# Two modulation blocks move from the out projection into the FFN up projection, with a new order of the first weight sums and activation sums

## The chip, the cores and the metric

The kernel runs on one core of one Trainium2 chip. The metric is the time on the device of one execution, in microseconds, as the median of several runs. The core has five engines with an instruction stream each: TensorE (PE, matrix products), VectorE (DVE), ScalarE (ACT), GpSimd (POOL) and SyncE (SP, which here only issues transfers). They wait for one another through semaphores. An engine takes its own stream in order, so whatever stands behind a waiting instruction waits as well.

## The reference

One decoder layer on a sequence of 1024 tokens of width 1024, in float32. A conditioning vector `c` gives six vectors of 1024 numbers each, by one product with `w_mod`:

```python
c_act = jax.nn.silu(c)
mod = c_act @ w_mod[l] + b_mod[l]
sh1, sc1, gt1, sh2, sc2, gt2 = [m[:, None, :] for m in jnp.split(mod, N_MOD, axis=-1)]
h = rms_norm(x, norm_mix[l]) * (1.0 + sc1) + sh1
p = h @ w_in[l]                      # split to three head groups: gMLP, RG-LRU, RWKV-7
y = jnp.concatenate([y_a, y_b, y_c], axis=-1) @ w_out[l]
x = x + gt1 * y
h = rms_norm(x, norm_ffn[l]) * (1.0 + sc2) + sh2
x = x + gt2 * conv_glu_ffn(h, ffn_w_up[l], ffn_conv_w[l], ffn_conv_b[l], ffn_w_down[l])
return rms_norm(x, norm_final)
```

`conv_glu_ffn` is `gate, val = split(h @ w_up)`, a causal convolution of three taps over time on `gate`, then `(silu(gate) * val) @ w_down`, with an inner width of 2816. The last modulation vector `gt2` is first read after the down projection's first product.

## The kernel before

**Precision.** Every float32 operand of a large product is split in two parts, a rounded one (`...h`, an ACT cast, L231) and the rest (`...l`, a DVE or POOL subtraction, L232). A product is three matmuls: high by high, high by low, low by high (L249 to L251, and L1124 to L1126 in the up projection). A matmul covers 128 x 128 weights and 512 tokens; the sequence is two halves f = 0 and 1 of 512 tokens (H).

**Modulation.** The product with `w_mod` is done in 12 blocks of 4 columns of `modc` each (`mod_block`, L279). A block has four loads of 512 KB (`wm`, L284). For each of the two halves of a load, DVE multiplies by a number of silu(c) and adds to `macc` (L292 for the first, L294 for the other seven); PE then sums over the partitions with four matmuls of one column (`pm`, L299), and DVE adds the bias (L300, `modc`). Blocks 4 to 9 are done inside the mixer. Blocks 10 and 11 give `gt2`, and wait in a list `modq`, four entries a block; `mod_rest(n)` takes the next n entries. A load takes one of three slots of the pool `wraw`, which the weights of the out projection, the up projection and `y` use as well. Slots are handed on in program order.

**Out projection.** For f = 0 and then 1, for 8 tiles k of the output (`out_tile`, L1027): x is loaded (L1029), the weights are loaded and split (`wr_wo`, `wh_wo`, `wl_wo`), 24 matmuls give `po`, DVE updates x (L1034), SP stores it (L1035), and ACT squares it for the next norm. `y_in` (L1018) loads what the mixer has stored (`yd`) and splits it. The table `MSTEP` says how many modulation entries run behind each of the 16 tiles: 4 for block 10 and 4 for block 11.

**FFN input.** `h2_in` (L1051) normalises x. The up projection multiplies 2 x 2 blocks (two halves of the tokens, two halves of the inner dimension) with seven products in place of eight, for tiles 1 to 21; tile 0 is done plainly. For that, sums of activation blocks T1 to T4 are formed on DVE for four chunks q (L1065 to L1068: T1, T3, T2, T4), and each is split in its parts: T2, T1 and T4 in the same loop, T3 in a loop behind it. T1 needs no T4; T2 is built on T1; T4 on T2.

**FFN up projection.** Each of 21 tiles has two raw weight blocks, `wr_ug` (gate) and `wr_uv` (value). `Up.first` (L1153) does the product `pA` with the block "11", and `gate` the product with "21", the convolution for f = 0 (`g`, L1141 to L1150). `Up.rest` (L1188) forms the weight sums in place, S3, S1, S2, S4 (L1201 to L1204, DVE or POOL by a table), splits them, and does the products `pB` (T2 by S2), `pD` (T3 by S3), `pC` (T1 by S1), `pD` again (T4 by v1) and `pC` again ("22" by S4): 84 matmuls a tile with `first` and `gate`. DVE reads the sums off PSUM: `p1` (L1211), `u` (L1214, L1218), `c` (L1221, L1222), `p1` again (L1225); the convolution for f = 1 follows, and two stores to `gd`. From tile 1 to 3, `first` has run before (NAHEAD = 3); tiles 4 to 20 ("late") have the gate's product between `pD` and `pC`.

**Order.** The code names the engine of each operation; a scheduler fixes each engine's order from the order of the code and its own estimates when the kernel is built. So a small edit moves instructions on every engine.

Of the kernel before, what the change touches and what calls it, by code (L numbers as in the profile page):

```python
# [14 lines left out]
ALU = mybir.AluOpType  # L15
# [6 lines left out]
H = 512  # L22
# [27 lines left out]

NAHEAD = 3
MAP = False
MSTEP = (0, 0, 0, 0, 0, 0, 1, 0, 1, 0, 0, 2, 1, 2, 0, 1)
FBLK = [(0, 4), (4, 10), (10, 16), (16, 18), (18, 22)]
NF2 = 3
NT2, NTB, _ = 7, 9, 5
# [96 lines left out]
def trunk(ctx: ExitStack, tc: tile.TileContext, xT, wmod, w_in, w_out, w_up, w_down,  # L153
          par, const, sgu_ln, sgu_wT, sgu_b, lora, g2w, lruw, outT):
    nc = tc.nc
    V, A, G, T = (Ordered(tc, e) for e in (nc.vector, nc.scalar, nc.gpsimd, nc.tensor))
    SY = nc.sync
# [69 lines left out]
    def eng(key, d):  # L227
        return {"V": V, "G": G, "A": A}[ENG.get(key, d)]
# [79 lines left out]
    yd = drp.tile([KT, P, S], F32, name="yd")  # L308
# [213 lines left out]
    def tb(nm):  # L522
        return r2.tile([P, H], F32, tag="tb", name=nm, bufs=NTB)

    def yout(kt, f, src):
        SY.dma_start(yd[kt, :, f * H:f * H + H], src)


    def c_tile(f, wi, idx, o, nm):
# [20 lines left out]
    def rwkv(j, f, stages):  # L550
# [13 lines left out]
        k = c_tile(f, 2 + 3 * j, 3 + j, t2(f"k{n}"), f"k{j}")  # L564
# [205 lines left out]
        def finish():  # L770

            mv = r1.tile([P, 3, 8], F32, tag="mv", name=f"mv{n}")
            sq = r2.tile([P, 8, 64], F32, tag="o", name=f"osq{n}", bufs=1)
            m_, s_, rs = mv[:, 0, :], mv[:, 1, :], mv[:, 2, :]
            V.reduce_sum(m_.unsqueeze(2), O, mybir.AxisListType.X)
            V.tensor_scalar(m_, m_, 1.0 / 64, None, ALU.mult)
            V.tensor_tensor(O, O, m_.unsqueeze(2).broadcast_to([P, 8, 64]), ALU.subtract)
            A.activation(sq, O, AF.Square)
            V.reduce_sum(s_.unsqueeze(2), sq, mybir.AxisListType.X)
            V.tensor_scalar(rs, s_, 1.0 / 64, GN_EPS, ALU.mult, ALU.add)  # L780
            rs = rsqrt(rs, 8, f"o{n}")
            yield
            eng("on", "V").tensor_tensor(O, O, rs.unsqueeze(2).broadcast_to([P, 8, 64]), ALU.mult)
            ps = mp.tile([P, 4, 2, 64], F32, tag="m", name=f"po{n}")
            for i in range(4):
                T.transpose(ps[:, i, :, :].rearrange("p a b -> p (a b)"),
                            O[:, 2 * i:2 * i + 2, :].rearrange("p a b -> p (a b)"), ident)
            o = r2.tile([P, H], F32, tag="o", name=f"o{n}", bufs=1)
            for hh in range(2):
                r_ = slice(64 * hh, 64 * hh + 64)  # L790
                for par_ in range(2):
                    A.activation(ch(o)[r_, par_:8:2, :], ps[64 * par_:64 * par_ + 64, :, hh, :], AF.Identity,
                                 scale=col("rwkv_ln_w", j)[r_], bias=col("rwkv_ln_b", j)[r_])
            eng("obv", "V").tensor_tensor(o, o, bv, ALU.add)
            ps = mp.tile([P, H], F32, tag="m", name=f"pgt{n}")
            T.matmul(ps, g2s[:, jc], sgg, start=True, stop=True)
            V.tensor_tensor(o, o, ps, ALU.mult)
            yout(5 + j, f, o)
            yield

        stages.update({f"L{j}{f}": lanes(), f"M{j}{f}": chain(), f"E{j}{f}": finish()})
# [208 lines left out]
    x1 = [[None] * KT, [None] * KT]  # L1010
# [31 lines left out]
    def parts(key, q, src, new, sh=None):  # L1042

        hi, lo = B[key, q] = tuple(new(f"{key}_{q}{p}") for p in "hl")
        if sh is None:
            split(src, hi, lo, eng("l" + key, "V"))
        else:
            A.activation(hi, src, AF.Identity, bias=sh)
            V.scalar_tensor_tensor(lo, src, sh, hi.bitcast(F32), ALU.add, ALU.subtract)

    def h2_in(f, acc):  # L1051

        rb = sumsq_bcast(acc, mp, f1, "rb", f"n2{f}", 1)
        yield
        hn = x1[f]
        sh = [modc[:, 24 + k:25 + k] for k in range(KT)]
        for q in range(4):
            for i, new in enumerate((hnew, hnew) if f == 0 else (anew, gnew)):
                k = q + 4 * i
                V.scalar_tensor_tensor(hn[k], hn[k], sg2[:, k:k + 1], rb, ALU.mult, ALU.mult)  # L1060
                parts(f"{i + 1}{f + 1}", q, hn[k], new, sh[k])
                yield
        for q in range(4 * f):
            b11, b21, b12, b22 = x1[0][q], x1[0][q + 4], hn[q], hn[q + 4]
            eng("T1", "V").tensor_tensor(b11, b12, b11, ALU.subtract)  # L1065
            eng("T3", "G").tensor_tensor(b12, b22, b12, ALU.subtract)
            eng("T2", "V").tensor_tensor(b22, b22, b11, ALU.subtract)
            eng("T4", "G").tensor_tensor(b21, b21, b22, ALU.subtract)  # L1068
            parts("T2", q, b22, anew, sh[q + 4])
            parts("T1", q, b11, anew)  # L1070
            parts("T4", q, b21, gnew)
            yield
        for q in range(4 * f):
            parts("T3", q, hn[q], anew, dsh[:, q:q + 1])
            yield
# [17 lines left out]
    for k in range(KT):  # L1093
        sq0 = out_tile(0, k, acc2[0])
        if k == 5:
            y_in(1)
        mod_rest(MSTEP[k])
    for k in range(KT):
        sq1 = out_tile(1, k, acc2[1])
        if k == 1:  # L1100
            h2 = h2_in(0, sq0)
            next(h2)
        mod_rest(MSTEP[8 + k])
        for _ in range((0, 1, 1, 2, 2, 2, 0, 0)[k]):
            next(h2)
    rp.close()
# [8 lines left out]
    def accp(nm):  # L1115
        return next(turn).tile([P, H], F32, tag="acc", name=nm)
# [15 lines left out]

    class Up:
        def __init__(self, ft):
            self.ft, self.raw = ft, None

        def conv(self, f, src):
            ft = self.ft
# [46 lines left out]
            V.tensor_tensor(g, g, ps[1], ALU.mult)  # L1185
            SY.dma_start(gd[ft, :, f * H:f * H + H], g)

        def rest(self, late):  # L1188
            ft = self.ft
            g = self.raw or raw_in(ft, f"ub{ft}")  # L1190
            v = raw_in(FT + ft, f"uv{ft}")
# [14 lines left out]
            wparts("S3", g0)  # L1206
            wparts("S1", v0)
            wparts("S4", g1)
            psB, psD, psC = accp(f"pB{ft}"), accp(f"pD{ft}"), accp(f"pC{ft}")
            prod(psB, w["S2"], "T2", True)  # L1210
            V.tensor_tensor(self.p1, self.p1, psB, ALU.add)  # L1211
            prod(psD, w["S3"], "T3", True)
            u3 = f2(f"u3{ft}")
            V.tensor_tensor(u3, self.p1, psD, ALU.add)  # L1214
            if late:
                self.gate()
            prod(psC, w["S1"], "T1", True)
            V.tensor_tensor(u3, u3, psC, ALU.add)  # L1218
            prod(psD, w["v1"], "T4", False)
            c21 = f2(f"c21{ft}")  # L1220
            V.tensor_tensor(c21, self.p1, psD, ALU.add)  # L1221
# [36 lines left out]
    for i in range(1, NAHEAD + 1):  # L1258
        ups[i].first(False, True)
        next(h2)  # L1260
    for _ in h2:
        pass
    for i in range(1, FT):
        late = NAHEAD < i < FT - 1
        if i > NAHEAD:
            ups[i].first(True, not late)
        ups[i].rest(late)
    fa = {}
    for b, (g0, g1) in enumerate(FBLK):
        last = b == len(FBLK) - 1  # L1270
# [136 lines left out]
```

## Time and profile before

| | us |
|---|---|
| median of 3 runs | 1378.88 |
| lowest and highest run | 1377.09, 1379.15 |
| the profiled execution, its own time | 1379.3 |
| its span in the profile | 1377.5 |
| PE busy | 1255.0 (91% of the span) |
| DVE busy | 896.3 (65%) |
| ACT busy | 583.7 (42%) |
| POOL busy | 335.8 (24%) |

All times of rows are microseconds from the start of the span. The busy share is an average over stages: the mixer ends near 580, the out projection runs to about 672, the up projection from there to about 1130, the down projection to the end. The "clock" of a stretch is the TensorE clock that was granted, as a share of full speed: 1.00 is 2.4 GHz, 0.50 is 1.2 GHz. A matmul's row tells when it starts and how long it is under way; matmuls overlap, so their price is the distance of their starts.

### The profile page before, as it was taken

What the parts mean: (1) busy time and instruction counts of PE and PEld (TensorE: products, weight loads), DVE (VectorE), ACT (ScalarE), POOL (GpSimd) and SP (SyncE); (2) the same over time, 40 slices, a digit from 0 to 9 for tenths busy, and PEclk for the clock granted to TensorE, in tenths of its full rate; (3) what the DMA queues carried; (4) which work ended last, traced back from release to release, by engine and by line L of the source; (5) the groups of instructions that cost most, each with busy time, mean ns of one, the idle gap of its engine ahead of it and who ended that gap; (6) DMA issues with size and microseconds to landing.
All of it is one profiled execution on the core that took longest, in us unless ns stands there. A gap on an engine that the chain in (4) does not pass through costs nothing. (4 is left out here: it accounts for less than half of the span.)

```text
span 1377.5 us, 18630 instructions
## 1 busy us (share of the span) xinstructions
PE 1255.0 (91%) x6948; PEld 1026.9 (75%) x6948; DVE 896.3 (65%) x1667; ACT 583.7 (42%) x1008; POOL 335.8 (24%) x294
## 2 busy tenths in 40 slices
PE   3778999888998979999979899999999999999996
PEld 3566878667686767778757788888888888888885
DVE  6778765755668484467697766666566575432566
ACT  4364655854655366333363333434434342110231
POOL 6674423206125220000001433332333200000000
PEclk9899999979999997899998999999999999999998
DMA  7453251433314243296413322232222374321213
GB/s 283 156 169 100 56 165 54 120 117 85 83 48 112 63 121 116 86 301 204 129 61 99 100 82 72 84 92 84 91 67 81 126 249 138 88 78 52 80 54 122
DMA packets 87498, 153.89 MB, mean 112 GB/s; under 512 B 37616, under 2 KB 39280, under 8 KB 87408
## 3 DMA queue, kind: packets, MB, share of 16 engines
q1 hardware_dynamic: 87408, 152.71, 35.6%
q8 instruction: 54, 0.88, 0.3%
q14 instruction: 36, 0.29, 0.1%
HBM read 126.60 MB, written 26.08 MB: 111 GB/s over the span
## 5 line engine op out<-in xcount | busy, mean ns | idle before, releaser
L1249 DVE SCALAR_TENSOR_TENSOR x<-pd,modc,x 128x512 f32<-128x512 f32 x80 | 59.6, 749 | 85.4 <-PE pd L251 85.3
L290 POOL TENSOR_TENSOR macc<-macc,wm 128x512 f32<-128x512 f32 x35 | 47.1, 1345 | 67.9 <-ACT wm L288 65.7
L231 ACT CAST wh_wd<-wr_wd 128x768 fp32r<-128x768 f32 (+2 forms) x32 | 21.7, 678 | 95.9 <-PE pd L250 94.0
L1202 POOL TENSOR_TENSOR wr_uv<-wr_uv 128x512 f32<-128x512 f32 x3 | 4.5, 1516 | 227.4 <-DVE wr_ub L1201 227.4
L1296 POOL TENSOR_TENSOR x<-x,rb_n 128x512 f32<-128x512 f32 x2 | 3.0, 1515 | 217.3 <-ACT rb_n L273 217.3
L232 DVE TENSOR_TENSOR wl_ug<-wr_ug,wh_ug 128x1024 fp32r<-128x1024 f32 x22 | 26.9, 1224 | 38.9 <-ACT wh_ug L231 38.7
L1227 POOL TENSOR_TENSOR u<-u,g 128x512 f32<-128x512 f32 x21 | 27.7, 1321 | 92.8 <-ACT g L1150 92.8
L758 DVE TENSOR_SCALAR U<-q,rn 128x64 f32<-128x64 f32 x48 | 13.4, 279 | 48.9 <-PE q L746 41.7
L231 ACT CAST wh_ug<-wr_ug 128x1024 fp32r<-128x1024 f32 x22 | 23.2, 1054 | 48.3 <-PE pA L1125 35.6
L627 PE MATMUL pg<-KGd,KB 128*128 128x128 f32 x192 | 31.4, 309 | 8.4 <-DVE KGd L612 6.0
L766 ACT COPY O<-q 128x64 f32<-128x64 f32 x48 | 10.1, 210 | 66.4 <-PE q L746 66.1
L746 PE MATMUL q<-SS,KGd 128*128 128x64 f32 x180 | 37.2, 291 | 0.0
L1211 DVE TENSOR_TENSOR p<-p,pB 128x512 f32<-128x512 f32 x21 | 14.4, 686 | 34.9 <-PE pB L1126 34.9
L746 PE MATMUL q<-VV,SCd 128*128 128x64 f32 x192 | 35.5, 289 | 0.2
L627 PEld LDWEIGHTS pg<-KGd,KB 128*128 128x128 f32 x192 | 27.4, 216 | 9.9 <-DVE KGd L612 6.7
L1150 ACT ACTIVATE g<-g 128x512 f32<-128x512 f32 x44 | 27.9, 634 | 13.1 <-DVE g L1145 13.1
L746 PEld LDWEIGHTS q<-VV,SCd 128*128 128x128 f32 x192 | 30.3, 205 | 3.9 <-issue 1.1
L1143 DVE SCALAR_TENSOR_TENSOR g<-p,pr,g 128x511 f32<-128x511 f32 (+1 forms) x42 | 33.2, 790 | 0.0
L1143 DVE SCALAR_TENSOR_TENSOR g<-pA,pr,g 128x511 f32<-128x511 f32 (+1 forms) x42 | 31.2, 744 | 2.9 <-ACT g L1141 2.6
L288 ACT ACTIVATE wm<-wm,cs 128x512 f32<-128x512 f32 x35 | 24.1, 719 | 15.9 <-DMA wm<-in_wmod_dram 14.1
L1204 POOL TENSOR_TENSOR wr_ug<-wr_ug,wr_uv 128x512 f32<-128x512 f32 x18 | 29.9, 1663 | 1.4
L746 PEld LDWEIGHTS q<-SS,KGd 128*128 128x128 f32 x180 | 29.7, 207 | 0.5 <-issue 0.5
(5035 smaller groups left out, 4446.3 us busy)
## 6 DMA issues: line engine op xcount, KB each, us to landing
wm<-in_wmod_dram SPq DMA_DIRECT2D x48, 512.0 KB, 4.1
wr_ug<-in_w_up_dram SPq DMA_DIRECT2D x22, 512.0 KB, 3.6
wr_uv<-in_w_up_dram SPq DMA_DIRECT2D x22, 512.0 KB, 3.6
wr_g<-gd SPq DMA_DIRECT2D x22, 512.0 KB, 3.3
x<-in_xT_dram SPq DMA_DIRECT2D x32, 256.0 KB, 5.5
wr_wo<-in_w_out_dram SPq DMA_DIRECT2D x16, 512.0 KB, 4.2
wr_wd<-in_w_down_dram SPq DMA_DIRECT2D x16, 384.0 KB, 3.1
gd<-c SPq DMA_DIRECT2D x21, 256.0 KB, 2.0
```

Source lines behind the costliest of these rows:

```text
L231: A.copy(hi, src)
L232: (e or V).tensor_tensor(lo, src, hi.bitcast(F32), ALU.subtract)
L288: A.activation(acc if k == 0 else wt[:, j, :], wt[:, j, :], AF.Copy, scale=cs[:, k:k + 1])
L290: G.tensor_tensor(acc, acc, wt[:, j, :], ALU.add)
L627: T.matmul(pg[hh][:, c, :, :], KB[:, 4 * g + c, :, :].rearrange("p a b -> p (a b)"), KG[g][:, c, :, r_], start=True, stop=True)
L746: T.matmul(o, w, x, start=start, stop=True, skip_group_check=True)
L1143: V.scalar_tensor_tensor(g[:, d:H], src[:, 0:H - d], taps[2 - d], g[:, d:H], ALU.mult, ALU.add)
L1150: A.activation(g, g, AF.Silu)
L1204: eng("S4" + e, "G").tensor_tensor(g1, g1, v1, ALU.subtract)
L1211: V.tensor_tensor(self.p1, self.p1, psB, ALU.add)
L1227: eng("c22", "V").tensor_tensor(u3, u3, g1_, ALU.mult)
L1249: V.scalar_tensor_tensor(x, ps, modc[:, 40 + k:41 + k], x, ALU.mult, ALU.add)
```

## The change

Five edits:

1. `MSTEP` goes, with its two calls. Blocks 10 and 11 now run whole, as `mod_rest(4)`, after the up projection's tiles 9 and 13.
2. In `h2_in` for f = 1, one loop forms T1, T3 and T2 and the parts of T1 and T2; a second forms T4 and its parts; T3's parts follow.
3. The weight sums of `Up.rest` become a method `prep`, and tile 1's is called before the loops of T4 and T3.
4. In tiles that are not late (1, 2, 3 and 21) the product T1 by S1 comes before T3 by S3, and `u` is first `p1 + pC`, then `+ pD`.
5. The last of the mixer's stores to `yd` is issued from ACT's queue in place of SP's.

```diff
--- before.py
+++ after.py
@@ -50,7 +50,6 @@
 
 NAHEAD = 3
 MAP = False
-MSTEP = (0, 0, 0, 0, 0, 0, 1, 0, 1, 0, 0, 2, 1, 2, 0, 1)
 FBLK = [(0, 4), (4, 10), (10, 16), (16, 18), (18, 22)]
 NF2 = 3
 NT2, NTB, _ = 7, 9, 5
@@ -522,8 +521,8 @@
     def tb(nm):
         return r2.tile([P, H], F32, tag="tb", name=nm, bufs=NTB)
 
-    def yout(kt, f, src):
-        SY.dma_start(yd[kt, :, f * H:f * H + H], src)
+    def yout(kt, f, src, q=SY):
+        q.dma_start(yd[kt, :, f * H:f * H + H], src)
 
 
     def c_tile(f, wi, idx, o, nm):
@@ -795,7 +794,7 @@
             ps = mp.tile([P, H], F32, tag="m", name=f"pgt{n}")
             T.matmul(ps, g2s[:, jc], sgg, start=True, stop=True)
             V.tensor_tensor(o, o, ps, ALU.mult)
-            yout(5 + j, f, o)
+            yout(5 + j, f, o, nc.scalar if (j, f) == (2, 1) else SY)
             yield
 
         stages.update({f"L{j}{f}": lanes(), f"M{j}{f}": chain(), f"E{j}{f}": finish()})
@@ -1065,9 +1064,12 @@
             eng("T1", "V").tensor_tensor(b11, b12, b11, ALU.subtract)
             eng("T3", "G").tensor_tensor(b12, b22, b12, ALU.subtract)
             eng("T2", "V").tensor_tensor(b22, b22, b11, ALU.subtract)
+            parts("T1", q, b11, anew)
+            parts("T2", q, b22, anew, sh[q + 4])
+            yield
+        for q in range(4 * f):
+            b21, b22 = x1[0][q + 4], hn[q + 4]
             eng("T4", "G").tensor_tensor(b21, b21, b22, ALU.subtract)
-            parts("T2", q, b22, anew, sh[q + 4])
-            parts("T1", q, b11, anew)
             parts("T4", q, b21, gnew)
             yield
         for q in range(4 * f):
@@ -1094,13 +1096,11 @@
         sq0 = out_tile(0, k, acc2[0])
         if k == 5:
             y_in(1)
-        mod_rest(MSTEP[k])
     for k in range(KT):
         sq1 = out_tile(1, k, acc2[1])
         if k == 1:
             h2 = h2_in(0, sq0)
             next(h2)
-        mod_rest(MSTEP[8 + k])
         for _ in range((0, 1, 1, 2, 2, 2, 0, 0)[k]):
             next(h2)
     rp.close()
@@ -1132,7 +1132,7 @@
 
     class Up:
         def __init__(self, ft):
-            self.ft, self.raw = ft, None
+            self.ft, self.raw, self.wr = ft, None, None
 
         def conv(self, f, src):
             ft = self.ft
@@ -1185,7 +1185,7 @@
             V.tensor_tensor(g, g, ps[1], ALU.mult)
             SY.dma_start(gd[ft, :, f * H:f * H + H], g)
 
-        def rest(self, late):
+        def prep(self):
             ft = self.ft
             g = self.raw or raw_in(ft, f"ub{ft}")
             v = raw_in(FT + ft, f"uv{ft}")
@@ -1206,16 +1206,28 @@
             wparts("S3", g0)
             wparts("S1", v0)
             wparts("S4", g1)
+            self.wr = w
+
+        def rest(self, late):
+            ft = self.ft
+            if self.wr is None:
+                self.prep()
+            w = self.wr
             psB, psD, psC = accp(f"pB{ft}"), accp(f"pD{ft}"), accp(f"pC{ft}")
             prod(psB, w["S2"], "T2", True)
             V.tensor_tensor(self.p1, self.p1, psB, ALU.add)
-            prod(psD, w["S3"], "T3", True)
             u3 = f2(f"u3{ft}")
-            V.tensor_tensor(u3, self.p1, psD, ALU.add)
             if late:
+                prod(psD, w["S3"], "T3", True)
+                V.tensor_tensor(u3, self.p1, psD, ALU.add)
                 self.gate()
-            prod(psC, w["S1"], "T1", True)
-            V.tensor_tensor(u3, u3, psC, ALU.add)
+                prod(psC, w["S1"], "T1", True)
+                V.tensor_tensor(u3, u3, psC, ALU.add)
+            else:
+                prod(psC, w["S1"], "T1", True)
+                V.tensor_tensor(u3, self.p1, psC, ALU.add)
+                prod(psD, w["S3"], "T3", True)
+                V.tensor_tensor(u3, u3, psD, ALU.add)
             prod(psD, w["v1"], "T4", False)
             c21 = f2(f"c21{ft}")
             V.tensor_tensor(c21, self.p1, psD, ALU.add)
@@ -1258,6 +1270,8 @@
     for i in range(1, NAHEAD + 1):
         ups[i].first(False, True)
         next(h2)
+    next(h2)
+    ups[1].prep()
     for _ in h2:
         pass
     for i in range(1, FT):
@@ -1265,6 +1279,8 @@
         if i > NAHEAD:
             ups[i].first(True, not late)
         ups[i].rest(late)
+        if i in (9, 13):
+            mod_rest(4)
     fa = {}
     for b, (g0, g1) in enumerate(FBLK):
         last = b == len(FBLK) - 1
```

Three places in the order of instructions follow. The line numbers in rows of the changed kernel are those of its own file.

SP's queue in the second half of the out projection, before; `wr_wo` are this stage's weights, `wm` the modulation loads, all in the pool of three slots:

```order
L241 DMA wr_wo_5690<-in_w_out_dram 128x1024
L1035 DMA x1d<-x_12_5530 128x512
L284 DMA wm_1_5726<-in_wmod_dram 128x1024
L1035 DMA x1d<-x_13_5573 128x512
L284 DMA wm_2_5730<-in_wmod_dram 128x1024
L241 DMA wr_wo_5746<-in_w_out_dram 128x1024
L1035 DMA x1d<-x_14_5635 128x512
L241 DMA wr_wo_5784<-in_w_out_dram 128x1024
L1035 DMA x1d<-x_15_5688 128x512
L284 DMA wm_3_5819<-in_wmod_dram 128x1024
L241 DMA wr_ug_5872<-in_w_up_dram 128x1024
L241 DMA wr_uv_5878<-in_w_up_dram 128x1024
```

The same place after the change:

```order
L240 DMA wr_wo_5710<-in_w_out_dram 128x1024
L1034 DMA x1d<-x_12_5521 128x512
L240 DMA wr_wo_5748<-in_w_out_dram 128x1024
L1034 DMA x1d<-x_13_5564 128x512
L240 DMA wr_ug_5826<-in_w_up_dram 128x1024
L1034 DMA x1d<-x_14_5612 128x512
L240 DMA wr_uv_5832<-in_w_up_dram 128x1024
L1034 DMA x1d<-x_15_5660 128x512
```

The modulation loads have gone from between the weight loads, and the first weights of the up projection follow directly.

DVE just ahead of tile 1's first product, before; `wr_uv<-wr_uv,wr_ub` is S2 and `wr_ub<-wr_ub,wr_uv` S3, `x_0` and `x_1` hold the sums, and `T_` parts with `dsh` are T3's:

```order
L1143 SCALAR_TENSOR_TENSOR g_6187<-pA_6160,pr,g_6187 128x511
L1068 TENSOR_TENSOR x_07_5378<-x_07_5378,x_17_5782 128x512
L1143 SCALAR_TENSOR_TENSOR g_6187<-pA_6160,pr,g_6187 128x510
L1049 SCALAR_TENSOR_TENSOR T_3l<-x_17_5782,modc,T_3h 128x512
L232 TENSOR_TENSOR T_3l<-x_03_5181,T_3h 128x512
L232 TENSOR_TENSOR T_3l<-x_07_5378,T_3h 128x512
L1049 SCALAR_TENSOR_TENSOR T_0l<-x_10_5415,dsh,T_0h 128x512
L1201 TENSOR_TENSOR wr_ub_6242<-wr_ub_6242,wr_uv_6244 128x512
L1049 SCALAR_TENSOR_TENSOR T_1l<-x_11_5456,dsh,T_1h 128x512
L1203 TENSOR_TENSOR wr_uv_6244<-wr_uv_6244,wr_ub_6242 128x512
L1049 SCALAR_TENSOR_TENSOR T_2l<-x_12_5530,dsh,T_2h 128x512
```

The same place after the change, where L1072 is T4's subtraction:

```order
L1072 TENSOR_TENSOR x_04_5219<-x_04_5219,x_14_5612 128x512
L1072 TENSOR_TENSOR x_05_5257<-x_05_5257,x_15_5660 128x512
L1143 SCALAR_TENSOR_TENSOR g_6131<-pA_6104,pr,g_6131 128x511
L1203 TENSOR_TENSOR wr_uv_6162<-wr_uv_6162,wr_ub_6160 128x512
L1143 SCALAR_TENSOR_TENSOR g_6131<-pA_6104,pr,g_6131 128x510
L1204 TENSOR_TENSOR wr_ub_6160<-wr_ub_6160,wr_uv_6162 128x512
L231 TENSOR_TENSOR S21l<-wr_uv_6162,S21h 128x512
L231 TENSOR_TENSOR T_0l<-x_04_5219,T_0h 128x512
L231 TENSOR_TENSOR S31l<-wr_ub_6160,S31h 128x512
```

S2 now stands ahead of two of T4's four subtractions, of all of T4's parts and of all of T3's, and S3 ahead of all four subtractions; S2's low part `S21l` comes directly behind S4.

DVE at the end of tile 9, before; `S310l` is the low part of tile 10's S3, and S3 and S1 of tile 10 stand some rows earlier:

```order
L1221 TENSOR_TENSOR c_7278<-p_7176,pD_7205 128x512
L1222 TENSOR_TENSOR c_7278<-c_7278,g_7246 128x512
L1225 TENSOR_TENSOR p_7176<-p_7176,pC_7206 128x512
L232 TENSOR_TENSOR S310l<-wr_ug_7451,S310h 128x512
L1143 SCALAR_TENSOR_TENSOR g_7295<-p_7176,pr,g_7295 128x511
L1145 SCALAR_TENSOR_TENSOR g_7295<-cf_7250,pr,g_7295 128x1
L1143 SCALAR_TENSOR_TENSOR g_7295<-p_7176,pr,g_7295 128x510
```

The same place after the change; `wm_3` is the block's last load, and `wr_ug_7428` and `wr_uv_7449` are tile 10's weights:

```order
L1234 TENSOR_TENSOR c_7379<-c_7379,g_7347 128x512
L293 SCALAR_TENSOR_TENSOR macc_7405<-wm_3_7418,cs,macc_7405 128x512
L1237 TENSOR_TENSOR p_7277<-p_7277,pC_7307 128x512
L299 TENSOR_TENSOR modc<-pm_7422,pr 128x4
L231 TENSOR_TENSOR wl_ug_7430<-wr_ug_7428,wh_ug_7431 128x1024
L1143 SCALAR_TENSOR_TENSOR g_7396<-p_7277,pr,g_7396 128x511
L1145 SCALAR_TENSOR_TENSOR g_7396<-cf_7351,pr,g_7396 128x1
L1143 SCALAR_TENSOR_TENSOR g_7396<-p_7277,pr,g_7396 128x510
L1145 SCALAR_TENSOR_TENSOR g_7396<-cf_7351,pr,g_7396 128x2
L1201 TENSOR_TENSOR wr_ug_7428<-wr_ug_7428,wr_uv_7449 128x512
L1202 TENSOR_TENSOR wr_uv_7449<-wr_uv_7449 128x512
L231 TENSOR_TENSOR wl_ug_7577<-wr_ug_7575,wh_ug_7578 128x1024
```

Tile 10's low part `wl_ug` and its sums S3 and S1 now stand behind the block, behind `modc` (which reads PE's `pm`), and behind tile 9's convolution. At tile 13 the order is the same with tile 14.

## Rows read from the trace of the kernel before

**Rows 1.** Waits of PE, 560 to 800 us: engine, line, releaser; total us, times, longest.

```profile
PE pB L1124 <- ACT S21h L231: 9.2, 1, 9.2
PE pD L1124 <- DVE u L1214: 4.6, 2, 4.0
PE po L249 <- DVE x L1034: 4.1, 1, 4.1
PE po L249 <- ACT wh_wo L231: 3.2, 1, 3.2
```

**Rows 2.** Stretches: length, busy us (instructions) by engine, clock, DMA share, GB/s.

```profile
657.80:664.00 6.20, 6.18 (x15) 4.69 (x16) 4.06 (x5) 0.59 (x1) 0.00 (x0) 0.52 0.71 219
725.30:731.60 6.30, 6.06 (x13) 4.30 (x14) 3.64 (x6) 1.52 (x3) 0.00 (x0) 0.50 0.35 98
769.50:773.00 3.50, 3.48 (x8) 2.83 (x9) 1.52 (x3) 0.30 (x1) 0.00 (x0) 0.51 0.95 298
783.70:1100.00 316.30, 316.30 (x1397) 261.89 (x1396) 198.28 (x296) 123.31 (x196) 108.15 (x80) 1.00 0.27 88
```

**Rows 3.** Timeline, out projection: start, us, engine, line, operation [idle before, releaser].

```profile
642.15 0.95 PE L299 MATMUL pm<-ones,macc 128*128 128x1 f32 x8
...
652.77 0.33 SPq L241 DMA_DIRECT2D wr_wo<-in_w_out_dram  x1
...
657.82 0.80 PE L249 MATMUL po<-y10h,wh_wo 128*128 128x512 f32 x1 [3.22 <-ACT wh_wo L231]
```

**Rows 4.** Timeline, front of the up projection, tile 1.

```profile
715.73 0.39 PE L1126 MATMUL pA<-21_3h,wl_ug 128*128 128x512 f32 x1
...
719.55 1.28 DVE L232 TENSOR_TENSOR T_3l<-x,T_3h 128x512 fp32r<-128x512 f32 x2
...
720.75 0.74 DVE L1049 SCALAR_TENSOR_TENSOR T_0l<-x,dsh,T_0h 128x512 fp32r<-128x512 f32 x1
...
723.91 0.69 DVE L1203 TENSOR_TENSOR wr_uv<-wr_uv,wr_ub 128x512 f32<-128x512 f32 x1 [1.15 <-POOL wr_uv L1202]
...
727.19 0.80 PE L1126 MATMUL pB<-T_0h,S21l 128*128 128x512 f32 x1 [0.23 <-DVE S21l L232]
...
742.46 0.39 PE L1124 MATMUL pB<-T_0h,S22h 128*128 128x512 f32 x1
```

**Rows 5.** Timeline, tiles 3 and 4 of the up projection.

```profile
753.61 0.33 SPq L1130 DMA_DIRECT2D wr_uv<-in_w_up_dram  x1
...
761.14 2.35 POOL L1204 TENSOR_TENSOR wr_ug<-wr_ug,wr_uv 128x512 f32<-128x512 f32 x1
...
769.52 0.80 PE L1124 MATMUL pD<-T_0h,v13h 128*128 128x512 f32 x1 [4.04 <-DVE u L1214]
```

**Rows 6.** Timeline, tiles 8 to 11, steady state.

```profile
873.98 0.74 DVE L1143 SCALAR_TENSOR_TENSOR g<-p,pr,g 128x511 f32<-128x511 f32 x1
...
875.43 0.21 DVE L1145 SCALAR_TENSOR_TENSOR g<-cf,pr,g 128x2 f32<-128x2 f32 x1
...
883.84 1.23 DVE L232 TENSOR_TENSOR wl_ug<-wr_ug,wh_ug 128x1024 fp32r<-128x1024 f32 x1 [2.29 <-ACT wh_ug L231]
...
891.14 0.69 DVE L1225 TENSOR_TENSOR p<-p,pC 128x512 f32<-128x512 f32 x1 [0.99 <-PE pC L1126]
...
888.31 1.29 POOL L1203 TENSOR_TENSOR wr_uv<-wr_uv,wr_ug 128x512 f32<-128x512 f32 x1 [0.83 <-POOL v111l L232]
889.68 1.62 POOL L1204 TENSOR_TENSOR wr_ug<-wr_ug,wr_uv 128x512 f32<-128x512 f32 x1
...
893.66 0.39 PE L1124 MATMUL pB<-T_0h,S210h 128*128 128x512 f32 x1
```

**Rows 7.** Lines of DVE: operation, count | busy, mean ns | idle before, releaser.

```profile
L294 DVE SCALAR_TENSOR_TENSOR macc<-wm,cs,macc 128x512 f32<-128x512 f32 x21 | 15.7, 747 | 6.6 <-DMA wm<-in_wmod_dram 6.4
```

**Rows 8.** DMA issues of the page: KB each, us to landing.

```profile
wm<-in_wmod_dram SPq DMA_DIRECT2D x48, 512.0 KB, 4.1
wr_ug<-in_w_up_dram SPq DMA_DIRECT2D x22, 512.0 KB, 3.6
```

## The prediction

> **What bounds the kernel now.** I read the shares of the page first (PE is busy in 91% of the span), then PE's waits stage by stage, since a change can only win where PE waits and lose where it makes PE wait. Between 560 and 800 us four releasers hold nearly all of PE's idle time [rows 1]: 9.2 us before tile 1's first product `pB`, for the high part of S2; 4.6 us before `pD`, for DVE's `u`, of which 4.0 in tile 3; 4.1 and 3.2 us in the out projection. Third, the table of stretches [rows 2]: behind three of these waits PE runs at the lower of its two levels (clock 0.50 to 0.52, 1.2 GHz), for 6.2, 6.3 and 3.5 us. From 783.7 to 1100 us PE is busy in 316.30 of 316.30 us at clock 1.00, with 1397 matmuls: 0.226 us each, 19.0 us for a tile's 84. There DVE is busy 198.28 us, 63%. So the up projection's steady part is purely PE's, whereas its front and the second half of the out projection have holes.
>
> The profiled execution took 1379.3 us, 0.4 above the median of the runs; the sum is made against it.
>
> **1. The blocks leave the out projection.** The last weights `wr_wo` are issued only at 652.77, since the pool's three slots are shared with `wm` and that slot is freed by a multiply-add of block 11; PE stands 3.22 us for their high part [rows 3]. Without the loads in between, the slot is freed by the tile before, and I count the 3.2 us as gone. With it goes the slow stretch behind: 15 matmuls in 6.20 us [rows 2] would take 15 x 0.226 = 3.4, so 2.8. Two groups `pm` leave PE here, 0.95 each [rows 3], 1.9. Sum -7.9. Bounds: -1.9, if another late transfer or DVE takes the place of the wait, and -7.9. The wait of 4.1 us for x stays: DVE's order there is the same.
>
> **2. The store on ACT's queue.** SP gets past it some 3 us earlier and issues x's loads earlier; what PE waits for there is x's update on DVE, whose order is unchanged. ACT idles where it now issues. 0, bounds -0.5 to +0.5 (a DMA issue row is 0.33 us [rows 3], and one instruction changes queue).
>
> **3. Front of the up projection.** PE ends tile 3's gate at 715.73 and runs fully again with the third `pB` at 727.19, when S2's low part is there; S2 starts at 723.91, 1.15 us of that waiting for POOL's S1 [rows 4]. Behind S2 go two subtractions of T4, four parts of T4 and three parts of T3: at 0.60 us by starts (two in 719.55 to 720.75) and 0.66 for T3's, 1.2 + 2.4 + 2.0 = 5.6. S3 is formed several instructions earlier, which covers S1 on POOL: 1.15 more. S2 then starts at 717.2, and one instruction fewer lies between S2 and its low part: third `pB` at about 719.9, -7.3.
>
> What is late next is T3: from S2 to the last part of T3 stand 19 DVE instructions of about 0.62, so it is ready at 717.2 + 11.9 = 729.1. Then PE has 23 matmuls of the tile left, 5.2 us: tile 2 begins at 734.3 and not at 742.46 [rows 4], -8.2. PE does T2's and T1's products meanwhile; a slow clock behind the shortened wait lies mostly under T3's chain.
>
> Tile 2 gets a wait that it had not: S1 of tile 3 on POOL now stands behind tile 1's last product `u`, and DVE's queue behind S2 of tile 3 waits with it, `u + pD` among them; by the same way of counting about 2.3 us. In tile 3 PE waits until 769.52 for `u` [rows 5]. That chain starts when tile 4's value weights land, 753.61 + 3.6 [rows 5, 8] = 757.2, and lasts 12.3 us. They now land about 5.3 us earlier (8.2 won, less the new wait and what remains of the slot's queue), and the chain is about 2.8 shorter, because tile 5's low part `wl_ug` (1.23 [rows 6]) and the idle time before it stand behind the convolution now: PE resumes at about 761.4. By then it has 43 of tile 3's matmuls behind it, and not 36, seven of "22" having moved ahead: (769.52 - 761.4) + 7 x 0.226 = 9.7. The slow 3.5 us behind that wait [rows 2] cost about 1.7; the wait shrinks to about 1.7 us, so I take half, 0.8. Together -10.5, all three tiles in one (tile 3's figure contains the ones before). Bounds -6 (the new wait in tile 2 twice as long, and POOL's S4 at 2.35 us) and -13 (no new wait, no slow clock).
>
> **4. The blocks in the up projection.** A block brings eight multiply-adds of 0.75 [rows 7], 6.0 us of DVE, into a tile where DVE has 7 of 19.0 free. They fit, but the loads take three slots ahead of tile 10's weights, so the lead with which a tile's sums are prepared is used up. What then lies on PE's path, in the time of tile 9 and 10 before [rows 6]: the last multiply-add ends about where `p + pC` starts, 891.1; `pm` 0.95 (892.05); `modc` 0.2; `wl_ug` of tile 10 1.23 (893.5), until which PE has two matmuls of tile 10. The convolution's four instructions, 873.98 to 875.64, 1.66 (895.1); S3 and S1, 0.6 each by starts (896.4); on POOL, S2 1.29, `u` of tile 9 about as much, S4 1.62, low part of S2 about 1.3 (901.9). There the third `pB` of tile 10 starts. Before it was the third from 893.66, 894.1; three gate matmuls now stand ahead of it, 0.7: 894.8. So +7.1 with `pm` contained. PE has some 2 us idle before the third `pA` and 5 us before `pB`; behind waits of 3.2 to 9.2 us the slow stretches were 3.5 to 6.3 us long [rows 1, 2], a loss of half their length, 1.7 to 3.1. I take 2.0: +9.1. Tile 11's sums are ready long before PE is at them, so nothing spreads. Twice, +18.2. Bounds for one block: +3 (only `pm` and the wait for `wl_ug`) and +13 (DVE late by 2, POOL held up by 1, a slow stretch of 3.1).
>
> **A rule on DVE and POOL.** POOL's S4 took 2.35 us at 761.14, beside a crowded DVE, and 1.62 in the steady state [rows 5, 6]; in the steady stretch POOL's 80 instructions took 108.15 us [rows 2], 1.35 each, with DVE busy 63% beside them, so most were not held up. The Trainium skill, "SBUF — State Buffer", section "SBUF: two separate sides", says that DVE and GpSimd share a pair of ports by an exclusive lock, held for a whole instruction, and that the other engine is blocked fully meanwhile. By that rule each of the four POOL instructions of the block's chain could lose a DVE instruction, and the time would be that of the rival held up, below, 1386.5, and not the forecast's 1378.7; the trace bears it out at 761.14 and not in the mean of the steady stretch.
>
> **Sum.** -7.9 + 0 - 10.5 + 18.2 = -0.2: 1379.1 on the profiled execution, 1378.7 against the median.
>
> **Rivals.**
> - *The blocks are cheaper.* If DVE's free 7 us let the last multiply-add end 2 us before 891.1 and the clock stays up, a block costs 7.1 - 2 = 5.1, two 10.2: -8.2, 1370.7. For it: DVE has slack, and loads of 4.1 us [rows 8] are issued a tile ahead. Against: the third slot's load can start only when the block's first is consumed.
> - *The blocks' chain is held up (slower).* In tile 10, and again 14, POOL's four instructions run beside DVE's low parts and convolution. If each takes 0.7 more, as S4 did (2.35 against 1.62), a block costs 7.1 + 2.8 + 3.1 = 13.0, two 26.0: +7.6, 1386.5. It decides from a mean of about 1.7 us for these four on. Against: the mean of 1.35.
> - *The front gives back.* Waits for T3 in tile 1 and for S1 in tile 2 eat what S2 wins: -6 in place of -10.5, 1383.2. For it: DVE has the same work to do there, only in another order; against: DVE's own wait of 1.15 us vanishes.
> - *The change does nothing in the out projection* (another transfer comes as late): -1.9 in place of -7.9, 1384.7. Little speaks for it: SP's queue holds only stores between the weight loads now.
>
> **How the numbers follow.** Differences under 0.2%, 2.8 us, can't be told from none here. Forecast, with 1375 to 1383 as its own range: 0.44, of which faster 0.13, same 0.23, slower 0.08. Blocks cheaper: 0.25, faster. Held up: 0.17, slower. Front gives back 0.10 and out projection 0.04: slower 0.11, same 0.03. Faster 0.38, same 0.26, slower 0.36. The range leaves out a tenth on each side: below, cheap blocks together with the front's -13 give 1368; above, held-up blocks and half of the front's loss give 1389.
>
> **What would show it.** Right: no PE wait for `wh_wo` past 590 and a full clock there; tile 2's first `pB` some 8 us earlier relative to the out projection's end; two new PE waits of about 5 us on the low part of S2 in tiles 10 and 14, each with a slow stretch behind. Wrong: PE without a hole at tile 10, or holes in tiles 11 and 15 too; a wait on the third tile unchanged at 4 us; the new wait in tile 2 much longer than 2.3.

## The result and the profile after

The changed kernel takes 1399.09 us (median of 4 runs, 1397.40 to 1402.93), the kernel before 1377.99 beside it: ratio 1.016, 95% interval 1.0137 to 1.0183. It is 21 us slower. Forecast were 1378.7, and 1389 as the upper end.

The profiled executions differ by 18.1 us (spans of 1395.6 and 1377.5). I split this by the starts of PE's matmuls: the first of the second half of the out projection (`po<-y10h`), the first of tile 0 (`pg`), and the first `pB` of tiles 6 and 16. The mixer, in which PE, DVE, ACT and POOL run the same instructions in the same order in both kernels, ended 3.2 us earlier in this execution of the changed kernel; over all 16 profiled kernels it ends between 5.5 us earlier and 5.6 later than before, so it is left out of the account, and 18.1 + 3.2 = 21.3 is to be explained. The stages that the table leaves out differ by 0.1 us or less each.

| stage | before | after | difference | forecast |
|---|---|---|---|---|
| out projection, second half | 55.25 | 48.04 | -7.2 | -7.9 |
| front: tile 0 to `pB` of tile 6 | 144.64 | 143.40 | -1.2 | -10.5 |
| `pB` of tile 6 to `pB` of tile 16 | 190.40 | 219.94 | +29.5 | +18.2 |

PE's waits from 700 to 1000 us of the changed kernel (engine, line, releaser; total us, times, longest), which answer to [rows 1]:

```profile
PE pD L1124 <- DVE u L1230: 7.7, 2, 4.2
PE pA L1124 <- ACT p L1164: 4.2, 3, 2.8
PE pB L1126 <- POOL S214l L231: 3.5, 1, 3.5
PE pB L1124 <- ACT S21h L230: 3.1, 1, 3.1
PE pB L1126 <- POOL S210l L231: 2.7, 1, 2.7
PE pC L1124 <- ACT g L1150: 1.7, 2, 0.8
PE pA L1126 <- DVE wl_ug L231: 1.6, 2, 0.8
PE pC L1124 <- DVE u L1225: 1.6, 1, 1.6
PE pB L1124 <- ACT S210h L230: 1.5, 1, 1.5
```

The 9.2 us before tile 1 have become 3.1 (counted from tile 0's start, the third `pB` came 6.6 us earlier; 7.3 were forecast), and the 3.2 for `wh_wo` are gone. But the wait for `u` has grown from 4.6 to 7.7, and six kinds of wait at tiles 10, 11 and 14 are new; a like wait of 1.2 us in tile 15 lies behind 1000. The stretches with a reduced clock answer to [rows 2] (length, busy us by engine with counts, mean clock of the stretch, DMA share, GB/s):

```profile
647.00:662.50 15.50, 15.50 (x74) 12.94 (x72) 9.93 (x13) 5.49 (x7) 0.00 (x0) 1.00 0.57 183
709.00:713.20 4.20, 4.10 (x10) 2.83 (x11) 4.20 (x9) 2.34 (x6) 0.00 (x0) 0.59 0.01 4
739.00:742.80 3.80, 3.80 (x11) 2.98 (x12) 2.96 (x5) 1.63 (x4) 0.00 (x0) 0.61 0.21 27
758.80:763.20 4.40, 4.33 (x10) 3.46 (x11) 1.83 (x3) 0.62 (x1) 1.17 (x1) 0.50 0.60 231
882.20:886.40 4.20, 3.83 (x10) 2.53 (x10) 4.17 (x7) 2.48 (x4) 1.33 (x2) 0.62 0.29 116
889.40:892.60 3.20, 0.51 (x2) 0.08 (x1) 2.92 (x2) 1.39 (x3) 3.19 (x3) 0.60 0.21 82
892.60:897.30 4.70, 4.65 (x12) 3.70 (x13) 1.25 (x3) 0.50 (x1) 0.00 (x0) 0.55 0.63 211
```

The first row is the end of the out projection: PE full, clock 1.00. The next three lie behind the waits of tiles 1, 2 and 3, where before there were two; the last three behind the first block.

**The front.** Rows of tile 2 in the timeline of the changed kernel (start, us, engine, line, operation [idle before, releaser]), in order of time:

```profile
732.99 0.69 DVE L1228 TENSOR_TENSOR u<-p,pC 128x512 f32<-128x512 f32 x1 [1.29 <-DMA gd<-c]
...
733.24 0.62 ACT L1150 ACTIVATE g<-g 128x512 f32<-128x512 f32 x1
...
733.94 1.49 POOL L1239 TENSOR_TENSOR u<-u,g 128x512 f32<-128x512 f32 x1 [11.17 <-ACT g L1150]
...
734.20 2.31 DVE L231 TENSOR_TENSOR wl_ug<-wr_ug,wh_ug 128x1024 fp32r<-128x1024 f32 x1
...
735.38 2.24 POOL L1202 TENSOR_TENSOR wr_uv<-wr_uv 128x512 f32<-128x512 f32 x1
...
737.66 0.69 DVE L1203 TENSOR_TENSOR wr_uv<-wr_uv,wr_ub 128x512 f32<-128x512 f32 x1 [1.15 <-POOL wr_uv L1202]
...
738.27 0.68 DVE L1230 TENSOR_TENSOR u<-u,pD 128x512 f32<-128x512 f32 x1
...
739.00 0.50 PE L1124 MATMUL pD<-T_0h,v12h 128*128 128x512 f32 x1 [3.57 <-DVE u L1230]
```

PE waits for `u + pD`, a sum with no POOL input; DVE has it behind S2 of tile 3, S2 waits for POOL's S1, and S1 stands behind tile 1's product `u` by `g`. Further up, DVE stood 1.29 us until a store of `c` had landed; what that costs PE no run here prices. Something similar happens in tile 3, with the sums of tile 4:

```profile
741.38 0.33 SPq L1130 DMA_DIRECT2D wr_uv<-in_w_up_dram  x1
...
750.11 2.69 POOL L1239 TENSOR_TENSOR u<-u,g 128x512 f32<-128x512 f32 x1 [1.61 <-ACT g L1150]
...
752.75 1.30 POOL L1203 TENSOR_TENSOR wr_uv<-wr_uv,wr_ug 128x512 f32<-128x512 f32 x1
...
754.08 0.62 ACT L230 CAST S24h<-wr_uv 128x512 fp32r<-128x512 f32 x1 [4.05 <-POOL wr_uv L1203]
...
754.60 0.61 ACT L230 CAST S34h<-wr_ug 128x512 fp32r<-128x512 f32 x1
...
755.25 0.70 DVE L231 TENSOR_TENSOR S34l<-wr_ug,S34h 128x512 fp32r<-128x512 f32 x1 [3.01 <-ACT S34h L230]
...
755.87 1.75 DVE L231 TENSOR_TENSOR S14l<-wr_uv,S14h 128x512 fp32r<-128x512 f32 x1
...
758.14 0.68 DVE L1230 TENSOR_TENSOR u<-u,pD 128x512 f32<-128x512 f32 x1
...
758.87 0.79 PE L1124 MATMUL pD<-T_0h,v13h 128*128 128x512 f32 x1 [4.15 <-DVE u L1230]
```

Here ACT casts the high part of tile 4's S2 before that of S3, so DVE's low part of S3, which POOL does not touch, waits for POOL's S2 all the same: 3.01 us of idle DVE, and `u + pD` is behind it. POOL has S2 behind its product `u` of tile 2.

**The blocks.** The first block's loads and tile 10's weights in the changed kernel, on SP's queue and where ACT takes the value weights up:

```profile
831.95 0.33 SPq L283 DMA_DIRECT2D wm<-in_wmod_dram  x1
...
848.34 2.98 SPq L283 DMA_DIRECT2D wm<-in_wmod_dram  x2
...
870.61 0.33 SPq L283 DMA_DIRECT2D wm<-in_wmod_dram  x1
...
875.61 0.33 SPq L1130 DMA_DIRECT2D wr_ug<-in_w_up_dram  x1
...
877.18 0.33 SPq L1130 DMA_DIRECT2D wr_uv<-in_w_up_dram  x1
...
882.23 0.62 ACT L230 CAST v110h<-wr_uv 128x512 fp32r<-128x512 f32 x1 [1.05 <-DMA wr_uv<-in_w_up_dram]
```

The same cast in the kernel before:

```profile
866.43 0.62 ACT L231 CAST v110h<-wr_uv 128x512 fp32r<-128x512 f32 x1 [0.99 <-PE pC L1125]
```

From 851 us on three `wm` hold all three slots, until the block's multiply-adds, which begin at 869.3, free them one by one. So ACT waits for tile 10's value weights until 19.2 us behind tile 9's first `pB` (863.07); in the kernel before it had them 8.2 us ahead of that `pB` (874.62). The chain from there to PE, in tiles 9 to 11:

```profile
878.93 0.75 DVE L293 SCALAR_TENSOR_TENSOR macc<-wm,cs,macc 128x512 f32<-128x512 f32 x1
...
880.97 1.23 DVE L231 TENSOR_TENSOR wl_ug<-wr_ug,wh_ug 128x1024 fp32r<-128x1024 f32 x1
...
882.90 1.85 DVE L1143 SCALAR_TENSOR_TENSOR g<-p,pr,g 128x510 f32<-128x510 f32 x1
...
882.93 1.28 POOL L231 TENSOR_TENSOR v110l<-wr_uv,v110h 128x512 fp32r<-128x512 f32 x1 [16.99 <-ACT v110h L230]
...
885.52 0.69 DVE L1202 TENSOR_TENSOR wr_uv<-wr_uv 128x512 f32<-128x512 f32 x1
...
886.13 1.22 DVE L231 TENSOR_TENSOR wl_ug<-wr_ug,wh_ug 128x1024 fp32r<-128x1024 f32 x1
...
886.34 2.13 POOL L1203 TENSOR_TENSOR wr_uv<-wr_uv,wr_ug 128x512 f32<-128x512 f32 x1 [2.14 <-DVE wr_uv L1202]
...
890.89 1.70 POOL L231 TENSOR_TENSOR S210l<-wr_uv,S210h 128x512 fp32r<-128x512 f32 x1
...
892.65 0.79 PE L1126 MATMUL pB<-T_0h,S210l 128*128 128x512 f32 x1 [2.74 <-POOL S210l L231]
...
908.20 0.47 PE L1124 MATMUL pC<-22_0h,S410h 128*128 128x512 f32 x1 [0.84 <-ACT g L1150]
...
929.08 0.50 PE L1124 MATMUL pC<-22_0h,S411h 128*128 128x512 f32 x1 [1.59 <-DVE u L1225]
```

The chain is link by link that of the prediction, 2.3 us later at its end: a convolution instruction took 1.85 us beside POOL's 1.28 (0.74 otherwise), S2 on POOL 2.13 and not 1.29 [rows 6], the low part 1.70. And it does not end at `pB`: `pC` waits in tile 10 and in tile 11.

### The profile page after: what moved, and what is told of

The parts are those of the page before. It is cut to its first block, busy times and chain, and to the rows that moved or that the text cites. A ratio compares the mean times of both kernels' runs of the same rounds, so it can differ in the third digit from the quotient of the medians.

```text
span 1395.6 us, 18604 instructions
## 1 busy us (share of the span) xinstructions
PE 1263.4 (91%) x6948; PEld 1029.2 (74%) x6948; DVE 914.3 (66%) x1667; ACT 581.6 (42%) x1008; POOL 342.7 (25%) x294
## 5 line engine op out<-in xcount | busy, mean ns | idle before, releaser
L1239 POOL TENSOR_TENSOR u<-u,g 128x512 f32<-128x512 f32 x21 | 30.7, 1462 | 117.1 <-ACT g L1150 117.1
L231 DVE TENSOR_TENSOR wl_ug<-wr_ug,wh_ug 128x1024 fp32r<-128x1024 f32 x22 | 30.9, 1404 | 22.6 <-ACT wh_ug L230 22.5
L1203 POOL TENSOR_TENSOR wr_uv<-wr_uv,wr_ug 128x512 f32<-128x512 f32 x18 | 24.8, 1380 | 21.0 <-issue 7.3
```

## The experiments

Theory S: the blocks cost what they do because their four loads take the slots ahead of the next tile's weights, so that its sums come too late. Theory D: DVE's added 6 us a block and the mutual slowing of DVE and POOL cost it, wherever the loads land. Theory P: the front gives its gain back through POOL's instructions in DVE's and ACT's queues; its rival, that DVE's own work bounds the front.

All figures of stages below are counted as in the table above, against the kernel before; the medians are of runs beside it on the same chip. Where one run is given, its total says little, because the mixer alone moves by more than most effects, and the stages decide.

**e1, blocks only.** `MSTEP` and its calls removed, and in the loop of the up projection of the kernel before:

```diff
         ups[i].rest(late)
+        if i in (9, 13):
+            mod_rest(4)
```

> Only the two modulation blocks are moved (behind tiles 9 and 13 of the up projection); the front and the store stay as in the kernel before. Theory S (the blocks' loads take the three slots ahead of the next tile's weights; from the profile after, out projection -7.2 and blocks +29.6): 1378 - 7.2 + 29.6 = about 1400. The sizes of the prediction (-7.9 and +18.2): about 1388.

1401.54 us; ratio 1.0163 (1.0126 to 1.0199). Out projection -7.2, front +0.3, blocks +29.7. The loss is the blocks'.

**e2, front only.** The changed kernel with `MSTEP` and its calls as before and without `mod_rest(4)` in the loop.

> The blocks stay in the out projection; the new order of T1 to T4, of tile 1's weight sums and of the products, and the store on ACT's queue are made. From the profile after (front -1.2): 1377, no difference that can be told. The prediction's size (-10.5): 1367.5.

1378.15 beside 1379.87; ratio 0.9975 (0.9955 to 0.9996). Front -2.4. The two waits for `u` in tiles 2 and 3 are there: 6.9 us.

**e3, a buffer of their own.** The moved blocks load into one tile of another pool:

```diff
-        ... bufs=NAHEAD + 1), wmtile, mp, MAP)] * 4]
+        ... bufs=NAHEAD + 1), lambda nm: wmo[0].tile([P, 2, H], F32, tag="wmo", name=nm, bufs=1), mp, MAP)] * 4]
```

> The changed kernel, but the moved blocks load into one buffer of their own and not into the three slots of the weights. DVE's eight multiply-adds a block and everything else stay. Theory S: the next tile's weights come as early as in the kernel before, PE's holes at tiles 10 and 14 go, and a block costs little more than its pm (1 us) and some 1 us of DVE: 1399 - 25 = about 1374. Theory D (DVE and POOL hold each other up, since DVE has 6 us more to do a block): the holes stay in great part, 1390 or more.

1380.01 beside 1379.87; ratio 1.0014 (0.9995 to 1.0033): between the two theories, nearer to S. The blocks fall from 29.5 to 11.7. The waits on tile 10's and 14's sums are gone; what is left stands in one row, PE's waits from 860 to 1000 us:

```profile
PE pm L298 <- DVE macc L293: 4.8, 2, 2.7
```

With a single buffer the four loads follow one another, and PE's `pm` waits in its queue for the last multiply-add, with tile 10's products behind it. The rest is `pm` itself and the slow clock behind each of the two waits.

**e4, no blocks.** Blocks 10 and 11 are left out; their columns of `modc` are zero.

> The changed kernel with blocks 10 and 11 left out altogether (the eight columns of modc are set to zero, so the output is not the reference's): it prices both blocks. From the profile after, tiles 10 to 12 and 14 to 16 lose 29.6 us: 1399 - 29.6 = about 1369.5. The sizes of the prediction: 1399 - 18.2 = 1381.

1371.46; ratio 0.9948 (0.9919 to 0.9976). Against the changed kernel's 1399.09 both blocks cost 27.6 us; by the stages, which leave the mixer out, 29.5 (tile 6 to 16 takes 190.40 us without them, as before).

**e5, own buffer and quarters.**

```diff
-        if i in (9, 13):
-            mod_rest(4)
+        if 6 <= i <= 13:
+            mod_rest(1)
```

> The changed kernel with the blocks' loads in a buffer of their own, and the blocks cut in quarters: one load and two multiply-adds behind each of tiles 6 to 13, pm behind the fourth. Theory S (slots, and PE waiting at pm for the last multiply-add): no holes at tiles 10 and 14, each block costs its pm of 1 us: 1371.5 + 2 = 1373.5. Theory D (any multiply-add on DVE in this stage costs PE time, because DVE and POOL hold each other up): 6 us of DVE a block cost the same wherever they stand, 1380 as with the own buffer and whole blocks.

1374.50 beside 1377.55; ratio 0.9984 (0.9962 to 1.0006). Blocks 4.4, of which the two `pm` are 1.9: the same 12 us of multiply-adds, in another place, cost PE little, which speaks against theory D as the main cause.

**e6, the front's S1 and `u` off POOL.** On top of e5, S1 and the products `u` by `g` of tiles 1 to 3 on DVE:

```diff
-ENG = {'s2':'G','KB1': 'V',
+ENG = {'s2':'G','S1e': 'V','KB1': 'V',
-            eng("c22", "V").tensor_tensor(u3, u3, g1_, ALU.mult)
+            (V if ft <= NAHEAD else eng("c22", "V")).tensor_tensor(u3, u3, g1_, ALU.mult)
```

> The kernel before this one (own buffer, quarters), with the sums S1 and the products u by g of tiles 1 to 3 on DVE in place of POOL. Theory P (the front gives its gain back because DVE's queue waits for POOL's S1 behind u in tile 2, and for S2 behind u in tile 3): the waits of PE before pD, 3.6 and 4.1 us, fall to under 2 in sum, and the two slow stretches behind them go: tile 4's first pB comes 5 to 9 us earlier, 1366. Rival (the front is bound by DVE's own work, of which this adds 5 us): no gain, 1373 or later.

1367.27; ratio 0.9932 (0.9908 to 0.9956). The waits for `u + pD` in tiles 2 and 3 fall from 6.9 in e5 to 1.5, the front from -2.6 to -6.5.

**e7, quarters in the shared slots.** The diff of e5 on the changed kernel.

> The changed kernel with the blocks in quarters behind tiles 6 to 13, but still in the three slots of the weights. Theory S: each load takes one slot and puts off the next tile's weights by part of a tile, so the holes are smaller but more: between 1374 and 1395, with the waits on tile 7 to 14's sums. If only whole blocks in a row hurt: 1373.

One run, 1377.88, with a mixer that ended 3.1 later than before's. Blocks 3.2. My theory S, in the form that each load in a slot puts off a tile's weights, is wrong: the slots cost next to nothing when the two weight loads of a tile stand between two `wm` on SP's queue, as they do here (`wm` at 780.56, 815.99, 824.21 and 838.39). It is the four loads in a row that use up the lead. The work itself is hardly spread: six of the first block's multiply-adds run between 818.5 and 831.0, in tile 6, and two in tile 7, where the changed kernel has eight in 10.4 us. So DVE's burst by itself is not what costs PE the 29 us.

**e8, POOL out of the block's chain.** `on = V if ft in (10, 14) else None`, taken for S2, S4 and the low parts.

> The changed kernel with S2, S4 and all low parts of the sums of tiles 10 and 14 on DVE: POOL leaves the chain behind the blocks. Theory S says the late weights are the cause and POOL's four instructions (1.3 to 2.1 us each in the profile after) only the last links: PE's third pB of tile 10 comes some 4 us earlier, both blocks 8 us less, 1391. Theory D (DVE and POOL hold each other up is the main cause): nearly all of the loss goes, 1375 to 1380.

One run, 1386.81. Blocks 20.6: with POOL out of the chain 8.9 of the 29.5 us go, as theory S had it (8), and 20.6 remain; tiles 11 and 15 still wait at `pC`, 2.2 and 2.6 us.

**e9, quarters, and the front's S1 and `u` on DVE.** The edits of e6 on e7, without a buffer of their own.

> Quarters behind tiles 6 to 13 in the three shared slots, with S1 and the products u by g of tiles 1 to 3 on DVE. If quarters need no buffer of their own (a quarter cost the same in e5 and e7 by the profiles), this equals the version with the own buffer: 1367, 0.7% under the kernel before. If the shared slots matter after all, 1369 to 1371.

1365.16 beside 1380.38; ratio 0.9883 (0.9841 to 0.9925). Out projection -7.2, front -7.6, blocks +3.2. It beats the kernel before and the changed one. Behind tile 21's first `pB` it loses 2.3 us: PE waits 1.96 us for `u + pD` there, since tile 21 has the new order of products too. That loss lies between 0.1 and 2.3 us in all kernels with the new order, and is 0.0 in e11, e12 and e14 and 0.3 in e1, which have the old one. PE's waits of over 1 us from 680 to 1000 us:

```profile
PE pB L1124 <- ACT S21h L230: 2.9, 1, 2.9
PE pC L1124 <- DVE u L1225: 2.5, 2, 1.5
PE pA L1124 <- ACT wh_ug L230: 1.5, 1, 1.5
PE pD L1124 <- DVE u L1230: 1.4, 2, 1.1
```

and in tile 21:

```profile
1100.01 0.50 PE L1124 MATMUL pD<-T_0h,v121h 128*128 128x512 f32 x1 [1.96 <-DVE u L1230]
```

**e10, only S1 on DVE**, on e7.

> As the quarters in the shared slots, and only S1 of tiles 1 to 3 on DVE; the products u by g stay on POOL. Theory P1 (POOL's S1 behind u is what tile 2 waits for, POOL's S2 behind u what tile 3 waits for): tile 2's wait before pD of 3.6 us falls under 1.5, tile 3's of 4.1 stays; about half of the front's 4.6 us. Rival: the product u by g on POOL is all of it: both waits stay.

One run, 1371.45. Front -4.1, from -1.9 in e7. As theory P1 had it, the wait for `u + pD` falls from 3.57 to 1.49 us in tile 2 and stays in tile 3 (3.39, then 3.53). So S1 is 2.2 us of it, and the products `u`, moved after it, another 3.5 (e9); the products alone were not tried.

**e11, the products in the old order**, on e7:

```diff
-            if late:
+            if True:
                 prod(psD, w["S3"], "T3", True)
                 V.tensor_tensor(u3, self.p1, psD, ALU.add)
-                self.gate()
+                if late:
+                    self.gate()
                 ...
```

> As the quarters in the shared slots, but tiles 1, 2, 3 and 21 do the product T3 by S3 before T1 by S1, as in the kernel before. It prices the swap of products. If T3's parts are the last to be ready in tile 1, PE waits for them here right behind pB, and tile 2 begins 2 to 4 us later than in the quarters' profile; if the swap only delays u, by which tiles 2 and 3 wait, these waits shrink by a product's 2.7 us and the two come out even.

One run, 1366.37, with a mixer 5.2 earlier. Front -3.3: tile 2 begins 1.9 us later than in e7, but its wait of 3.57 is gone, so neither of the two expected pictures came as it stood. The swap of products costs 1.4 us at the front as long as POOL is in the chains, and 1.2 in tile 21.

**e12, quarters alone**, on the kernel before.

> The kernel before with the two blocks in quarters behind tiles 6 to 13, and nothing else changed (front, products and store as before). From the profiles: out projection -7.2, quarters +3.2, so the down projection begins 4 us earlier, counted from the out projection's start: about 1374. With the front edits it was 1.2 to 2 us less.

One run, 1378.37, with a mixer 4.1 later. Out projection -7.2, blocks +1.9, from the second half of the out projection to the down projection -5.4 in all: 1.4 more than expected, since the blocks cost no more than their two `pm`.

**e13, only the products `u` of tiles 9 and 13 on DVE**, on the changed kernel.

> The changed kernel with whole blocks, and only the product u by g of tiles 9 and 13 on DVE, so that on POOL S4 and the low part of S2 of tiles 10 and 14 follow S2 directly. Theory Q (a place in a queue): the third pB of tiles 10 and 14 comes 1.3 us earlier each, the duration of one POOL product; both blocks about 27 us. Theory H (POOL and DVE lengthen each other's instructions beside each other): u moved to DVE lengthens as much as it saves, and the third pB comes within 0.5 us of the profile after.

One run, 1397.41, with a mixer 4.3 earlier and a first half of the out projection 3.7 longer, which the edit does not touch. Blocks 27.1, as theory Q says; but from tile 9's first `pB` to tile 10's third it is 28.74 us and not 29.58, 0.8 of the 1.3, and `u` took 1.76 us on DVE. Both have a part.

**e14, e9 with the old order of products.**

> The fastest version so far (quarters, S1 and the products u by g of tiles 1 to 3 on DVE), with the product T3 by S3 before T1 by S1 as in the kernel before. If the swap costs by itself (1.4 us in the quarters' profiles): 1364. If it cost only through POOL's waits, which are gone here, then T3's parts, last to be ready in tile 1, hold PE: 1366 to 1368.

1366.13 beside 1377.37; ratio 0.9911 (0.9878 to 0.9944). Front -6.0 and not -7.6: once this work is off POOL, the swap wins 1.6 us at the front. But tile 21 loses 2.3 by it, and the blocks cost 1.9 here and 3.2 in e9, which has a wait of 0.94 us in tile 9 that e14 lacks. From tile 0 to the down projection e14 is 1.9 us shorter than e9, in one profile each: nothing here shows that the swap pays on the whole. The medians of e9 and e14 are too near to tell them apart.

## Why the prediction was wrong, step by step

1. *The blocks leave the out projection*, -7.9: right. -7.2 in every kernel without them; clock 1.00, no wait for `wh_wo`. e2, which keeps them, shows 3.1 us of that wait.
2. *The store*, 0: the first half of the out projection takes 61.3 us and not 61.2. What it does to the end of the mixer can't be seen under the mixer's own spread: e1, with the old store, ends the mixer 4.5 us earlier than the kernel before, and e12 4.1 later.
3. *The front*, -10.5: wrong in its second half. The first steps held in kind: 3.1 us of wait are left before tile 1, tile 2 begins 6.5 us earlier (8.2 forecast). The step that failed is "PE resumes at about 761.4" in tile 3. Counted from tile 0's start it resumes 0.3 us earlier than before, not 8. Both parts of that step missed. Tile 4's value weights were to come 5.3 us earlier, and their load is issued 1.9 earlier, counted in the same way (741.38; 753.61 before [rows 5]): less was won ahead of tile 2, and the new wait there was longer. The chain from that load to PE was to be 2.8 us shorter, and is 1.6 longer. I had shortened that chain by counting DVE's rows alone, and had not followed ACT's queue (S3's high part behind S2's) nor POOL's (S2 behind `u`). In tile 2 the same kind of wait was seen, put at 2.3 and measured at 3.57, and its slow clock (739.0 to 742.8) not put down at all. e6, e9 and e10 show POOL's part: with S1 and the products `u` on DVE the front gives 6.5 to 7.6. The 3 to 4 us that are still missing from 10.5 are not settled by a run. The rival "the front gives back" was the case, with -1.2 in place of its -6.
4. *The blocks*, +18.2: right in sign and mechanism, too small by 11.3. For one block: the third `pB` of tile 10 was put at +7.1 and came at 9.4 (29.58 us behind tile 9's first, 19.49 before, less 0.7 for the three gate matmuls ahead); the clock was put at 2.0, and from that `pB` on 12 matmuls at 0.55 (892.6 to 897.3) cost 4.7 - 2.7 = 2.0, as said. "Tile 11's sums are ready long before, so nothing spreads" is the failed step: `pC` waits 0.84 us in tile 10 and 1.59 in tile 11, 2.4 in sum. 9.4 + 2.0 + 2.4 = 13.8 of the 14.5 measured for this block. The reason for the 2.3 us at `pB` is, by the rows, the rival's "held up": convolution 1.1, S2 0.8, low part 0.4 longer; S4 was 0.4 shorter than put down, and the chain up to `wl_ug` 0.3 longer. POOL's four instructions took 1.59 us on the mean in tile 10 and 1.74 in tile 14, and the rival's sign was about 1.7. The mean of 1.35 us, which I held against it, was of tiles in their usual order; behind a block both engines have the late tile's sums to do at once. That this is why they meet is argued from the rows. The rule of the Trainium skill, "SBUF — State Buffer", section "SBUF: two separate sides", on the lock that DVE and GpSimd share, bears on the same rows: S2 on POOL, which began 0.2 us behind `wl_ug` (1.22 us) on DVE, took 2.13. The rows agree with it; the lock itself is argued, not shown.

Three of the prediction's own signs of being wrong are in the trace: holes in tiles 11 and 15, a wait of some 4 us in tile 3 as before, and a new wait in tile 2 well over 2.3.

The two errors point the same way, and add up to 20.6 us: 9.3 at the front and 11.3 at the blocks. The out projection adds 0.7.

## What to carry to other kernels

A gain at the head of a chain is worth what the next chain lets through: follow each engine's queue, not only the data, since the sum that PE waited for needed nothing of POOL and still stood behind it. Work that fits an engine's free time by its sum can still hurt if its loads come in one go and use up the buffers that keep the next stage ahead: in quarters, in the same buffers, the same work cost 2 to 3 us and not 29. A reordering that wins in one place also runs wherever else the code uses it: the swap of products won at the front and lost in tile 21. A mean duration from a stretch where two engines take turns doesn't hold where they meet.

## What the runs showed of the hardware

The granted clock fell to its lower level (0.50, 1.2 GHz) behind waits of PE of 2.7 to 4.2 us as it did behind 9.2: the stretches shown have means of 0.50 to 0.61. In tile 10 it fell as well behind `pm` with waits of 0.3 us ahead of it and 0.8 us soon after (mean 0.62 from 882.2 to 886.4). It stayed at 1.00 behind the waits of 0.84 and 1.59 us at `pC` (908.2 to 912.0, 929.1 to 933.0). DVE instructions on tiles of 128 x 512 took 1.75 to 1.85 us in place of 0.68 to 0.74, and POOL's 2.13 to 2.69 in place of 1.3, in places where the two ran beside each other; in other such places one of the two, or neither, took longer. The mixer's end moved by 11 us between executions of kernels with the same mixer, more than most of the effects that were looked for; stages of the profile told apart what medians could not.
